# A four-layer fp32 trunk: the pairs' loads in another order, the first layer's squares and the last weights at other places

## Chip, cores, metric

The kernel runs on one core of a Trainium2 chip. The metric is the device time of one execution in microseconds; of several runs the median counts. The engines are called as the profile calls them: PE is TensorE's matmuls (PEld its weight loads), DVE is VectorE, ACT ScalarE, POOL GpSimd, SP SyncE, which here only issues DMAs.

## The reference

One batch of 512 tokens with 1024 channels passes through four residual layers (pool, conv, multi-head latent attention, pool), all in float32. Cut to what matters:

```python
for i in range(4):
    kind, j = i % 3, i // 3
    if kind == 0:
        x = x + pool_mixer(rms_norm(x, pool_norm[j]), ...)
    elif kind == 1:
        x = x + conv_mixer(rms_norm(x, conv_norm[j]), ...)
    else:
        x = x + mla_mixer(rms_norm(x, mla_norm[j]), cos, sin, ...)
return rms_norm(x, final_norm)

def pool_mixer(xn, w_in, w_grp, scale, w_out):
    u, z = split(xn @ w_in, 2)
    ...
    pooled.append(mean - u[:, :, g])
    ...
    mixed = einsum('bsgc,gcd->bsgd', pooled, w_grp) * scale
    return (mixed * silu(z)) @ w_out

def conv_mixer(xn, w_in, conv_w, w_out):
    b, c, h, z = split(xn @ w_in, 4)
    y = b * causal_conv3(c * h, conv_w)
    return (y * silu(z)) @ w_out
```

u, z, b, c and h have 2048 columns each. mean is the trailing mean over the last 2, 4, 8 or 16 tokens, by the column group g.

## The kernel before

**Products.** A matrix product in float32 is made of three matmuls of a shorter type: each operand is split into a high part (a rounded copy, made by ScalarE) and a low part (operand minus high part, made by VectorE), and high x high, high x low and low x high are summed. Names end in h and l for the two parts: wr is a raw block of weights from a DMA, wh and wl are its parts; xh and xl those of the normalised input; yh and yl those of a layer's inner result.

**Jobs.** The work of a layer is a list of jobs (class Stream, L185 to L231). Most jobs load 128x1024 weights, split them (prepare_chunk, L238) and run 24 matmuls of 512 columns: a tile job, for example the u tiles of the pool layers. The other kind is a *pair* (L386 to L460): two tiles of the output from seven products instead of eight, each a product of 12 matmuls of 256 columns. The seven products (function seven, L429) run in the order A11, S1, A22, A12, S2, S4, S3, and need these split weights: ah, al (from the raw block r) for A11 and A22; sh, sl (from s13) for S1 and S3; ch, cl (from r4) for A12; th, tl (from r and r4 after the sums L399 and L400) for S2 and S4. In between, parts of the results are copied out of the accumulators (kept, L440).

A pair's raw data are r (128x1024), r4 (128x512) and s13. s13 is a sum: two loads of the same 128x512 columns into its two halves, and then a DMA on GpSimd's queue that adds the 128x1024 of r's source to it in memory (L120). r and s13 take buffers from the pool "wr", which has four and which also serves the weights of the tile jobs; r4 takes one of two in "wq". A load whose buffer is still in use waits on SyncE's queue, and all loads behind it with it.

**What sets the order.** Inside a stream the order of TensorE, VectorE and ScalarE is the order in which the program issues (tc.manual_schedule, L227); the orders of SyncE and GpSimd are chosen by a scheduler. A job has eight positions, 0 to 7, for a pair the gaps ahead of its products. Steps (functions to be run at a position) are kept in a table (class Steps, L164); a position of 8 or more runs over into the next job. While job j runs, the loads of jobs j+1 and j+2 are issued at its start, and the steps that prepare job j+1's weights lie at its positions: for a pair (L406) 4 ah, 5 al and sh, 6 sl and ch, 7 cl and the sums, 10 th, 11 tl. The steps that take a finished tile further (posts) go to the following jobs. The last pool layer runs its list up to its last eight jobs with all engines' orders left to the scheduler (L1241), and the rest by hand.

**The normalisation.** The input's root mean square is worked out beside the products and applied behind them, as a factor R per token. For it the squares of the eight x tiles are made on ScalarE (L276), summed on GpSimd (the last one on VectorE, L282), closed (split), and turned into the factors by rows (TensorE, VectorE), diagonal (VectorE) and bcast (TensorE), then copied to R (L322). In class Layer (L464) two numbers (at) say after which finished tile rows is put in line, and after which R is made. No tile of the layer can be finished before R is there. A pair needs, beside xh and xl, sums of their halves, the forms (L351): per two x tiles four operations on VectorE (d, L363 to L366), two copies on ScalarE (fh) and two subtractions on VectorE (fl, L382); each forms has its own position.

**The first layer** (pool) starts with two tiles whose matmuls go along with the arrival of x (first_two, L1120). The squares of all eight x tiles then lie in the job behind (positions 0 to 7), close at 10, the four forms at 24, 40, 56 and 72 from there on. rows comes after the fourth tile, R after the sixth (at=(4, 6), L1151). A u tile's post adds shifted copies on GpSimd (L617), up to four of them, then hd, mean and the rest on VectorE (L623 to L625), then a split (plh, pll).

**The end.** The last matrix, pool_out1, is used token-major. Its first column half runs in the last jobs of the stream (token_major, last_half). For its second half four blocks of weights are loaded (L1249) and split into eight parts (wres, L1251 through split, L155 to L162) behind the last job, and then four token tiles follow (L1252 and on), each with its square sums, final norm and its output DMAs.

Of the kernel before, what the change touches and what calls it, by code (L numbers as in the profile page):

```python
# [9 lines left out]
F32 = mybir.dt.float32  # L10
# [6 lines left out]
P = 128  # L17
S = 512
# [46 lines left out]
def trunk_kernel(ctx: ExitStack, tc: tile.TileContext, a):  # L65
# [16 lines left out]
    def wt(s, tag, dt=F32R, w=CH):  # L82
        return wp.tile([P, CH], dt, tag=tag, name=nm(s), bufs=BUFS[tag])[:, :w]
# [29 lines left out]
    def load_pair(src):  # L113

        r, r4, s13 = wt("wr", "wr", F32), wp.tile([P, S], F32, tag="wq", name=nm("wq"), bufs=2), wt("s13", "wr", F32)
        nc.sync.dma_start(r, src[:, :CH])
        nc.sync.dma_start(r4, src[:, CH + S :])
        for q in range(2):
            nc.sync.dma_start(s13[:, q * S : (q + 1) * S], src[:, CH : CH + S])
        nc.gpsimd.dma_start(s13, src[:, :CH], accum_op=ALU.add)  # L120
        return r, r4, s13

# [62 lines left out]
    class Stream:  # L185
# [3 lines left out]
        def __init__(self):  # L189
            self.jobs, self.at, self.later, self.raw, self.ready = [], 0, Steps(), {}, {}  # L190

# [3 lines left out]
        def load(self, j):  # L195
            if j < len(self.jobs) and j not in self.raw:
                kind, src, _ = self.jobs[j]
                self.raw[j] = kind[0](src) if kind else None

# [14 lines left out]
        def step(self):  # L214
            j = self.at
            self.at += 1
            self.load(j + 1)
            self.load(j + 2)
            now, self.later = self.later, Steps()
            now.put(self.prepare(j + 1), 2 if self.jobs[j][0] is PAIR and self.jobs[j + 1 :] and self.jobs[j + 1][0] is not PAIR else 0, first=True)  # L220
            self.jobs[j][2](self.ready.pop(j, None), now)
            now(7)
            left, self.later = self.later, Steps()
            self.later.put(now.at, -8)
            self.later.put(left.at)
# [7 lines left out]
    def load_chunk(src, width=CH):  # L233
        raw = wt("wr", "wr", F32, width)
        nc.sync.dma_start(raw, src)
        return raw

# [14 lines left out]
    def wchunk(src, width=CH, pool=False):  # L252
        w, steps = prepare_chunk(load_chunk(src, width), width, pool)
        Steps(steps)(2)
        return w
# [864 lines left out]
    def first_two():  # L1120

        pre = [ps("pt") for _ in range(2)]
        for k in range(KD):
# [16 lines left out]
            for m in range(2):  # L1140
                wh, wl = w0[m, hf]
                if k == m == 0:
# [4 lines left out]
                    continue  # L1147
                mm3(pre[m], wh[:, c], wl[:, c], *xn0.xs[k], first=(k == 0), last=(k == KD - 1))

        for m in range(KD):  # L1150
            s1.later.put({m: [lambda m=m: xn0.st.add(xt[m])]})  # L1151
        s1.later.put({10: [xn0.st.close]})
        for kk in range(KK):
            s1.later.put(xn0.forms(kk), 24 + 16 * kk)
        return pre

    pool_layer(s1, 0, xn0, half, at=(4, 6), pre=first_two)
    xn = nxt
# [24 lines left out]

    def token_major(stream, c, hf, ys, then):

        pos = []

        def run(wl, now, kp):
            if kp == 0:
                pos.extend(ps("po") for _ in range(NT))  # L1190
# [16 lines left out]
    tail = {}  # L1207

    def last_half(hf, ys):
        if hf == 0:  # L1210
            for c in range(2):
                token_major(s2, c, 0, ys, add_tok)
        else:
            token_major(s2, 0, 1, ys, finish)
            tail["ys"] = ys
# [29 lines left out]
    ys = tail["ys"]  # L1245
    wres = {}
    for kk in range(4):
        raw = wt("wr", "wr", F32)
        nc.sync.dma_start(raw, w[1, 4 + kk])  # L1249
        for e in range(2):  # L1250
            wres[2 * kk + e] = split(raw[:, e * S : (e + 1) * S], "w")  # L1251
    for i in range(NT):  # L1252
# [116 lines left out]
```

## Time and profile before

| | |
|---|---|
| median of 3 runs | 1501.44 us (1498.50 to 1502.46) |
| the profiled execution | 1502.28 us |
| its span, first to last instruction | 1500.5 us |
| mean granted TensorE clock | 0.991 of full speed |
| busy: DVE, ACT, POOL | 1086.7, 686.9, 258.3 us |
| DMA | 181.71 MB, mean 121 GB/s |

The profile shows one execution. A line of the timeline reads: start and duration in us, engine, source line, operation, out<-in by the program's names (s stands for s13 as well as for the sums of the pool layers, since numbers are cut off), shape, and in brackets the idle time of the engine just before, with what ended it. A line of the waits reads: engine and line that waited, what it waited for, us in total, times, and the longest. A line of the windows reads: stretch, its length, busy time (and instructions) of PE, PEld, DVE, ACT and POOL, then the clock granted to TensorE as a share of full speed, the DMA engines' busy share, and GB/s.

### The profile page before, as it was taken

To read this page: it belongs to the slowest core of one execution; us is meant where nothing else is said; L and a number is where in the kernel's file an instruction comes from. 1 tells how busy PE (TensorE), PEld (TensorE's weight loads), DVE (VectorE), ACT (ScalarE), POOL (GpSimd) and SP (SyncE) were. 2 spreads that over 40 slices of the span, in tenths; PEclk is the share of its full clock that TensorE was granted. 3 is DMA by queue.
4 is the path that set the end of the run, shared out by engine and by line. 5 is a ranking of instruction groups with operands and counts; after the bars stand their busy time and mean duration, and the time that the engine had idled before them with its cause. 6 is when DMAs were issued, how large, how long until landed. Compare 5 with 4: busy or idle time off the path is not lost. (4 is left out here: it accounts for less than half of the span.)

```text
span 1500.5 us, 22412 instructions
## 1 busy us (share of the span) xinstructions
PE 1451.2 (97%) x8560; PEld 1273.3 (85%) x8560; DVE 1086.7 (72%) x1771; ACT 686.9 (46%) x1174; POOL 258.3 (17%) x291
## 2 busy tenths in 40 slices
PE   9999999999999999999999999999999999999997
PEld 7788797888999889999879988788888798888886
DVE  5885556659988878998688976667755487655854
ACT  4352233445554425555355655555633355323333
POOL 2413106021001000000211001121201122311502
PEclk9999999999999999999999999999999999999999
DMA  6243354325676457666236642122122434343431
GB/s 229 70 121 105 102 137 99 127 89 120 179 185 162 139 125 191 168 181 194 86 97 169 159 148 74 55 66 84 43 84 85 113 106 115 132 108 117 113 113 57
DMA packets 65147, 181.71 MB, mean 121 GB/s; under 512 B 8080, under 2 KB 8080, under 8 KB 65040
## 3 DMA queue, kind: packets, MB, share of 16 engines
q1 hardware_dynamic: 56688, 151.44, 31.7%
q0 software_dynamic: 7488, 27.27, 10.9%
q8 instruction: 67, 1.10, 0.3%
q10 hardware_dynamic: 864, 1.57, 0.3%
q14 instruction: 40, 0.33, 0.1%
HBM read 173.70 MB, written 2.10 MB: 117 GB/s over the span
## 5 line engine op out<-in xcount | busy, mean ns | idle before, releaser
L248 DVE TENSOR_TENSOR wl<-wr,wh 128x1024 fp32r<-128x1024 f32 (+1 forms) x140 | 173.1, 1236 | 55.9 <-ACT wh L245 54.7
L245 ACT ACTIVATE wh<-wr 128x1024 fp32r<-128x1024 f32 (+1 forms) x140 | 144.4, 1034 | 147.7 <-PE o L259 47.7
L260 PE MATMUL o<-yh,wl 128*128 128x512 f32 x384 | 151.3, 394 | 1.9 <-DVE wl L248 1.9
L259 PE MATMUL o<-yl,wh 128*128 128x512 f32 x384 | 151.3, 394 | 0.2 <-DVE yl L667 0.2
L258 PE MATMUL o<-yh,wh 128*128 128x512 f32 x384 | 150.9, 393 | 0.1
L260 PE MATMUL pt<-xh,wl 128*128 128x512 f32 x367 | 145.3, 397 | 4.0 <-DVE wl L248 4.0
L258 PE MATMUL pt<-xh,wh 128*128 128x512 f32 x367 | 146.2, 398 | 2.7 <-ACT wh L245 2.5
L259 PE MATMUL pt<-xl,wh 128*128 128x512 f32 x367 | 145.2, 396 | 0.6 <-DVE xl L349 0.6
L396 DVE TENSOR_TENSOR sl<-s,sh 128x1024 fp32r<-128x1024 f32 x52 | 65.4, 1259 | 35.2 <-ACT sh L393 32.8
L440 ACT ACTIVATE kept<-bv 128x256 f32<-128x256 f32 x52 | 19.9, 383 | 152.6 <-PE bv L426 90.7
L260 PEld LDWEIGHTS o<-yh,wl 128*128 128x128 f32 x384 | 72.1, 188 | 19.2 <-DVE wl L248 2.8
L260 PEld LDWEIGHTS pt<-xh,wl 128*128 128x128 f32 x367 | 69.5, 189 | 21.6 <-DVE wl L248 5.3
L259 PEld LDWEIGHTS o<-yl,wh 128*128 128x128 f32 x384 | 72.1, 188 | 17.2 <-DVE yl L667 0.5
L258 PEld LDWEIGHTS o<-yh,wh 128*128 128x128 f32 x384 | 72.1, 188 | 17.0 <-ACT yh L664 0.5
L258 PEld LDWEIGHTS pt<-xh,wh 128*128 128x128 f32 x367 | 69.5, 189 | 19.9 <-ACT wh L245 3.8
L259 PEld LDWEIGHTS pt<-xl,wh 128*128 128x128 f32 x367 | 69.5, 189 | 16.5 <-DVE xl L349 1.0
L120 POOL DMA_DIRECT2D s<-in_conv_in x30 | 26.0, 865 | 329.6 <-DMA s<-in_conv_in 105.4
L617 POOL TENSOR_TENSOR s<-u 128x527 f32<-128x527 f32 x32 | 50.0, 1562 | 180.6 <-DVE u L580 146.5
L282 POOL TENSOR_TENSOR sq<-sq,sq 128x512 f32<-128x512 f32 x25 | 39.6, 1585 | 211.3 <-ACT sq L276 210.9
L396 DVE TENSOR_TENSOR al<-wr,ah 128x1024 fp32r<-128x1024 f32 x52 | 64.1, 1233 | 14.2 <-ACT ah L393 12.1
L617 POOL TENSOR_TENSOR s<-s 128x525 f32<-128x525 f32 (+2 forms) x48 | 69.8, 1454 | 14.4 <-PE pm L259 11.1
L393 ACT ACTIVATE sh<-s 128x1024 fp32r<-128x1024 f32 x52 | 54.9, 1055 | 35.1 <-DMA s<-in_conv_in 17.8
(308 smaller groups left out, 4575.2 us busy)
## 6 DMA issues: line engine op xcount, KB each, us to landing
wr<-in_conv_in SPq DMA_DIRECT2D x34, 512.0 KB, 5.6
wr<-in_pool_out SPq DMA_DIRECT2D x32, 512.0 KB, 3.3
wr<-in_pool_u SPq DMA_DIRECT2D x30, 512.0 KB, 3.9
s<-in_conv_in SPq DMA_DIRECT2D x60, 256.0 KB, 4.6
s<-in_conv_in POOLq DMA_DIRECT2D x30, 512.0 KB, 6.2
wr<-in_pool_z SPq DMA_DIRECT2D x18, 512.0 KB, 4.0
wr<-in_pool_grp SPq DMA_DIRECT2D x16, 512.0 KB, 3.3
wr<-in_conv_out SPq DMA_DIRECT2D x16, 512.0 KB, 3.5
```

The source lines that it names most:

```text
L120: nc.gpsimd.dma_start(s13, src[:, :CH], accum_op=ALU.add)
L245: nc.scalar.activation(h, raw, AF.Copy)
L248: (nc.gpsimd if pool else nc.vector).tensor_tensor(out=l, in0=raw, in1=f(h), op=ALU.subtract)
L258: nc.tensor.matmul(out, ah, bh, start=first, stop=False)
L259: nc.tensor.matmul(out, ah, bl, start=False, stop=False)
L260: nc.tensor.matmul(out, al, bh, start=False, stop=last)
L282: eng.tensor_tensor(out=self.sum, in0=self.sum, in1=sq, op=ALU.add)
L393: return lambda: nc.scalar.activation(h, t, AF.Copy)
L396: return lambda: nc.vector.tensor_tensor(out=l, in0=t, in1=f(h), op=ALU.subtract)
L440: nc.scalar.activation(dst, src, AF.Copy)
L617: nc.gpsimd.tensor_tensor(out=nx[:, lo:], in0=cur[:, lo:], in1=cur[:, lo - d : S + PAD - d], op=ALU.add)
```

## The change

It has three parts.

1. **load_pair** issues s13's two loads first, then r and r4, and hands the summing DMA back as a step at position 4 of the job at whose start the loads are issued (Stream.loads), instead of issuing it at once.
2. **The first layer's squares**: first_two adds the square of x tile k-2 while tile k is worked on, the last two at position 0 of the job behind; close moves from position 10 to 3, rows and R one tile ahead (at=(3, 5)), the forms to 48, 56, 64 and 72.
3. **The last weights** (resident): the four loads and eight splits of wres lie at positions of the last four jobs of the stream (loads at 0 or 4, splits from 8, 10 or 12 on), instead of behind the last job. token_major calls resident at the start of each of its jobs, through a new last argument.

The core of the diff:

```diff
-        r, r4, s13 = wt("wr", "wr", F32), wp.tile([P, S], F32, tag="wq", name=nm("wq"), bufs=2), wt("s13", "wr", F32)
+        s13 = wt("s13", "wr", F32)
+        for q in range(2):
+            nc.sync.dma_start(s13[:, q * S : (q + 1) * S], src[:, CH : CH + S])
+        r, r4 = wt("wr", "wr", F32), wp.tile([P, S], F32, tag="wq", name=nm("wq"), bufs=2)
         nc.sync.dma_start(r, src[:, :CH])
         nc.sync.dma_start(r4, src[:, CH + S :])
-        for q in range(2):
-            nc.sync.dma_start(s13[:, q * S : (q + 1) * S], src[:, CH : CH + S])
-        nc.gpsimd.dma_start(s13, src[:, :CH], accum_op=ALU.add)
-        return r, r4, s13
+        return (r, r4, s13), {4: [lambda: nc.gpsimd.dma_start(s13, src[:, :CH], accum_op=ALU.add)]}
...
                 kind, src, _ = self.jobs[j]
-                self.raw[j] = kind[0](src) if kind else None
+                self.raw[j], steps = kind[0](src) if kind else (None, {})
+                self.loads.put(steps)
...
             self.load(j + 2)
             now, self.later = self.later, Steps()
+            now.put(self.loads.at)
+            self.loads = Steps()
...
                 mm3(pre[m], wh[:, c], wl[:, c], *xn0.xs[k], first=(k == 0), last=(k == KD - 1))
-
-        for m in range(KD):
-            s1.later.put({m: [lambda m=m: xn0.st.add(xt[m])]})
-        s1.later.put({10: [xn0.st.close]})
+            if k >= 2:
+                xn0.st.add(xt[k - 2])
+
+        for m in range(KD - 2, KD):
+            s1.later.put({0: [lambda m=m: xn0.st.add(xt[m])]})
+        s1.later.put({3: [xn0.st.close]})
         for kk in range(KK):
-            s1.later.put(xn0.forms(kk), 24 + 16 * kk)
+            s1.later.put(xn0.forms(kk), 48 + 8 * kk)
         return pre
 
-    pool_layer(s1, 0, xn0, half, at=(4, 6), pre=first_two)
+    pool_layer(s1, 0, xn0, half, at=(3, 5), pre=first_two)
     xn = nxt
...
+    wres = {}
+
+    def resident(now, kp):
+
+        for kk, n, at in ((0, 0, 8), (1, 0, 12), (2, 1, 12), (3, 2, 10)):
+            if n == kp:
+                raw = wt("wr", "wr", F32)
+                wres.update({2 * kk + e: (ut("wh", F32R), ut("wl", F32R)) for e in range(2)})
+                now.put({4 if kp else 0: [lambda raw=raw, kk=kk: nc.sync.dma_start(raw, w[1, 4 + kk])]})
+                for e in range(2):
+                    (h, l), half = wres[2 * kk + e], raw[:, e * S : (e + 1) * S]
+                    now.put({at + e: [lambda h=h, half=half: nc.scalar.activation(h, half, AF.Copy)],
+                             at + 2 + e: [lambda h=h, l=l, half=half: nc.vector.tensor_tensor(out=l, in0=half, in1=f(h), op=ALU.subtract)]})
+
     def last_half(hf, ys):
         if hf == 0:
             for c in range(2):
                 token_major(s2, c, 0, ys, add_tok)
         else:
-            token_major(s2, 0, 1, ys, finish)
+            token_major(s2, 0, 1, ys, finish, resident)
             tail["ys"] = ys
...
-    wres = {}
-    for kk in range(4):
-        raw = wt("wr", "wr", F32)
-        nc.sync.dma_start(raw, w[1, 4 + kk])
-        for e in range(2):
-            wres[2 * kk + e] = split(raw[:, e * S : (e + 1) * S], "w")
     for i in range(NT):
         b = slice(i * P, (i + 1) * P)
```

**SyncE in the conv layer.** Ahead of each step in the loop the loads of one pair are queued; wr is r, wq is r4. In the steady part of the conv layer, before:

```order
L116 DMA wr_976_5631<-in_conv_in 128x1024
L119 DMA s13_978_5633<-in_conv_in 128x512 x2
L117 DMA wq_977_5632<-in_conv_in 128x512
L116 DMA wr_995_5764<-in_conv_in 128x1024
L119 DMA s13_997_5766<-in_conv_in 128x512 x2
L117 DMA wq_996_5765<-in_conv_in 128x512
```

and now (line numbers of the changed file):

```order
L117 DMA s13_976_5631<-in_conv_in 128x512 x2
L119 DMA wr_977_5634<-in_conv_in 128x1024
L120 DMA wq_978_5635<-in_conv_in 128x512
L117 DMA s13_995_5764<-in_conv_in 128x512 x2
L119 DMA wr_996_5767<-in_conv_in 128x1024
L120 DMA wq_997_5768<-in_conv_in 128x512
```

s13 and r have changed places in the queue of SyncE; r4 stays the last.

**GpSimd in the first layer.** The summing DMAs of the first layer's last two pairs (s_402 and s_415, in the changed kernel s_400 and s_413) stand among the shifted adds of tiles u31, u32 and u33, four adds to a tile. Before:

```order
L617 TENSOR_TENSOR s_1994<-u_1984 128x527
L617 TENSOR_TENSOR s_1996<-s_1994 128x525
L617 TENSOR_TENSOR s_1998<-s_1996 128x521
L120 DMA s_402_2086<-in_pool_z 128x1024
L617 TENSOR_TENSOR s_2000<-s_1998 128x513
L610 MEMSET u_2081 128x16
L617 TENSOR_TENSOR s_2098<-u_2081 128x527
L617 TENSOR_TENSOR s_2100<-s_2098 128x525
L617 TENSOR_TENSOR s_2102<-s_2100 128x521
L120 DMA s_415_2137<-in_pool_z 128x1024
L617 TENSOR_TENSOR s_2104<-s_2102 128x513
```

and now:

```order
L620 TENSOR_TENSOR s_1954<-s_1952 128x521
L121 DMA s_400_2084<-in_pool_z 128x1024
L620 TENSOR_TENSOR s_1956<-s_1954 128x513
L613 MEMSET u_1984 128x16
L620 TENSOR_TENSOR s_1994<-u_1984 128x527
L620 TENSOR_TENSOR s_1996<-s_1994 128x525
L620 TENSOR_TENSOR s_1998<-s_1996 128x521
L620 TENSOR_TENSOR s_2000<-s_1998 128x513
L613 MEMSET u_2081 128x16
L121 DMA s_413_2135<-in_pool_z 128x1024
L620 TENSOR_TENSOR s_2097<-u_2081 128x527
```

The first of the two has moved ahead by a tile's adds, and the second stands ahead of its tile's first add instead of in front of the last.

**ScalarE in the last layer**, at its last pair but one (z30): ch, sh, th are the splits of the pair's weights, plh that of a u tile, yh that of an inner result, kept the copy behind the pair's second product, gf a load of the final gain. Before:

```order
L393 ACTIVATE sh_14233<-s_2686_14172 128x1024
L393 ACTIVATE ch_14231<-wq_14171 128x512
L628 ACTIVATE plh_14168<-s_14190 128x512
L664 ACTIVATE yh_14260<-E_13889 128x512
L440 ACTIVATE kept_14313<-bv_14310 128x256
L393 ACTIVATE th_14235<-wr_14170 128x512
```

and now:

```order
L396 ACTIVATE sh_14232<-s_2684_14170 128x1024
L443 ACTIVATE kept_14313<-bv_14310 128x256
L396 ACTIVATE th_14234<-wr_14173 128x512
L396 ACTIVATE ch_14230<-wq_14174 128x512
L631 ACTIVATE plh_14168<-s_14189 128x512
L667 ACTIVATE yh_14259<-E_13889 128x512
```

kept and the first th have moved ahead of ch, plh and yh.

More of the change, by code (lines that the diff above doesn't have):

```diff
@@ L189, in __init__ @@
         def __init__(self):
-            self.jobs, self.at, self.later, self.raw, self.ready = [], 0, Steps(), {}, {}
+            self.jobs, self.at, self.later, self.loads, self.raw, self.ready = [], 0, Steps(), Steps(), {}, {}
         def add(self, kind, src, run):
@@ L235, in load_chunk @@
         nc.sync.dma_start(raw, src)
-        return raw
+        return raw, {}
     def prepare_chunk(raw, width=CH, pool=False):
@@ L252, in wchunk @@
     def wchunk(src, width=CH, pool=False):
-        w, steps = prepare_chunk(load_chunk(src, width), width, pool)
+        w, steps = prepare_chunk(load_chunk(src, width)[0], width, pool)
         Steps(steps)(2)
@@ L1182, in trunk_kernel, with token_major @@
     w = a["pool_out1"]
-    def token_major(stream, c, hf, ys, then):
+    def token_major(stream, c, hf, ys, then, stay=None):
         pos = []
         def run(wl, now, kp):
+            if stay:
+                stay(now, kp)
             if kp == 0:
```

## The prediction

> **What bounds the kernel now.** I read the busy shares of the page first, then TensorE's waits, then the windows (for the granted clock), and last the timeline around each wait that the change can reach.
>
> ```profile
> span 1500.5 us, 22412 instructions
> PE 1451.2 (97%) x8560; PEld 1273.3 (85%) x8560; DVE 1086.7 (72%) x1771; ACT 686.9 (46%) x1174; POOL 258.3 (17%) x291
> 1440.00:1460.00 20.00, 20.00 (x88) 16.22 (x87) 8.39 (x10) 4.86 (x6) 0.00 (x0) 1.00 0.33 106
> ```
>
> TensorE is the bound: busy for 97% of the span. At its steady pace it starts 88 matmuls of 512 columns in 20 us, one each 0.23, so that a job of 24 lasts 5.5 us. The change leaves the matmuls as they are. It can win only the places where TensorE waits, and lose only by making new ones. Its parts reach four groups of waits: in the pairs of the conv and attention layers (380 to 900 us), in the first layer's opening (60 to 95), near 250, and near 1469. A fifth place, near 1414, has a changed order of ScalarE.
>
> **Part 1, the pairs' loads: s13 asked for ahead of r.** First TensorE's waits from 380 to 900 us on the tiles made of s13, then SyncE's waits for a buffer over the span, then one pair of the conv layer.
>
> ```profile
> PE bx L426 <- DVE tl L396: 3.0, 7, 1.0
> PE bv L426 <- DVE sl L396: 2.2, 3, 0.8
> PE bv L420 <- ACT sh L393: 1.8, 2, 1.0
> ...
> SPq L116 <- DVE wr L399: 170.2, 32, 10.6
> SPq L119 <- DVE tl L396: 84.6, 32, 4.7
> ...
> 411.11 0.86 POOL L120 DMA_DIRECT2D s<-in_conv_in  x1 [9.93 <-DVE cl L396]
> 411.47 0.33 SPq L116 DMA_DIRECT2D wr<-in_conv_in  x1
> 414.70 1.08 SPq L119 DMA_DIRECT2D s<-in_conv_in  x2
> 420.22 1.06 ACT L393 ACTIVATE sh<-s 128x1024 fp32r<-128x1024 f32 x1 [3.50 <-DMA s<-in_conv_in]
> 421.33 0.38 PE L420 MATMUL bv<-fh,sh 128*128 128x256 f32 x1 [0.78 <-ACT sh L393]
> 427.43 1.04 ACT L393 ACTIVATE ah<-wr 128x1024 fp32r<-128x1024 f32 x1
> ...
> 1412.66 0.28 PE L425 MATMUL bv<-fl,sh 128*128 128x256 f32 x1
> 1412.78 0.28 PE L426 MATMUL bv<-fh,sl 128*128 128x256 f32 x1
> ```
>
> The summing DMA of this pair's s13 went out at 411.11, and its sum was there when sh began at 420.22, 9.1 us later. ScalarE had then stood 3.50 for it, and TensorE 0.78 for sh. The three rows of waits give 7.0 us in 12 waits. Each understates its loss: steady matmuls of 256 columns start 0.12 apart and are recorded as 0.28 long (the last two rows, from a pair that nothing holds up), so a shown gap hides 0.16 more. That makes 7.0 + 12 x 0.16 = 8.9 us.
>
> In the loop r waits for a buffer until the sums of an earlier pair (L399) are done, s13 until its tl (L396), which comes later; here 411.47 against 414.70, 3.2 us apart. With s13 asked for first, the two trade places: s13 goes out about 3.2 us earlier and r about as much later. The longest stand of sh here, 3.50, then shrinks to some 0.3, and since TensorE stood only 0.78 of that, its wait goes. I keep 0.9 of the 8.9 for pairs where a sum is slow again: gain **8.0** (range 4 to 8.9).
>
> What the move costs: r is now the later of the two. It is first read by ah, at 427.43 for the r that would be asked for at 414.70, so it has 12.7 us.
>
> ```profile
> wr<-in_conv_in SPq DMA_DIRECT2D x34, 512.0 KB, 5.6
> DMA to landing us min/median/max: 5.4/6.2/9.1
> ```
>
> r lands in 5.6 us (first row); even the slowest summing DMA, of the same 512 KB, took 9.1 (second row). That leaves 3.6 us, so r's delay is hidden behind the products of the pair before, and costs nothing. If the cover were gone, ah would come late and with it the first product of each pair (a rival below). The summing DMA's later place in the program costs nothing either: GpSimd stands for s13's loads anyway, and in the conv layer its queue keeps its order.
>
> **Part 1 in the first layer, near 250.** GpSimd's queue among the adds for tile u32, VectorE's step behind them, TensorE's wait, and two windows (the granted clock is the third number from the end):
>
> ```profile
> 248.41 0.87 POOL L120 DMA_DIRECT2D s<-in_pool_z  x1 [1.93 <-DMA s<-in_pool_z]
> 250.64 0.17 DVE L623 TENSOR_TENSOR hd<-s,con 128x16 f32<-128x16 f32 x1 [4.48 <-POOL s L617]
> 254.49 0.39 PE L426 MATMUL bx<-xh,al 128*128 128x256 f32 x1 [3.26 <-DVE al L396]
> ...
> 254.98:258.40 3.42, 3.42 (x19) 3.42 (x18) 3.42 (x4) 0.63 (x1) 2.51 (x2) 0.50 0.00 0
> 380.00:690.00 310.00, 303.99 (x2358) 292.47 (x2358) 267.01 (x376) 157.09 (x257) 24.02 (x39) 1.00 0.64 167
> ```
>
> The summing DMA sits inside the adds and holds GpSimd for 1.93 until the loads have landed; hd, then al, then TensorE wait in a chain. In the changed order it stands ahead of these adds, with its loads asked for earlier. So hd comes 1.93 sooner and TensorE's wait falls from 3.26 to 1.3. The window behind the wait had a granted clock of 0.50 for 3.42 us, which costs 1.7. A wait of 2.06 near 1469 (below) was followed by such a window too, while the conv layer, 380 to 690, with single waits of up to 1.0 (above), kept 1.00. At 1.3 I take the clock to stay whole: gain 1.9 + 1.7 = **3.6** (range 1.9, if the clock still falls, to 5.1, if the whole wait goes). [...]
>
> **Part 2, the last weights.** Around the wait for their first split:
>
> ```profile
> 1445.84 1.21 DVE L248 TENSOR_TENSOR wl<-wr,wh 128x1024 fp32r<-128x1024 f32 x1
> 1469.42 7.03 DVE L161 TENSOR_TENSOR wl<-wr,wh 128x512 fp32r<-128x512 f32 x8 [0.37 <-ACT wh L158]
> 1469.44 1.52 PE L258 MATMUL po<-wh,yh 128*128 128x512 f32 x5 [2.06 <-ACT wh L158]
> ...
> 1470.13:1473.54 3.41, 3.17 (x10) 2.31 (x9) 3.41 (x4) 2.90 (x6) 2.16 (x2) 0.50 0.01 2
> ```
>
> The eight splits stand in a row behind the squares of the row sums (L1224), and TensorE waits 2.06 for the first, then runs 3.41 us at half clock (1.7). Moved into the last four jobs, they need 7.0 us of VectorE in a stretch where it is busy 8.39 of 20, and ScalarE 4.86 (window 1440 to 1460, above). They fit. Gain 2.06 + 0.16 + 1.7 = **3.9** (range 2.2, if the clock still falls for another reason, to 4.2). What they move back: on SyncE's queue two of the new loads now stand ahead of the chunk of the last job, which so waits for the buffer that the split at 1445.84 frees, until 1447. Its load, 512 KB like those above, would land by 1453; its job is the last of four of 5.5 us before 1465, so it has until 1460. Nothing is lost.
>
> **Part 3, the first layer's squares.** TensorE's waits from 60 to 95 us, a window, and VectorE's rows:
>
> ```profile
> PE pt L260 <- DVE wl L248: 3.2, 2, 2.4
> PE pt L258 <- ACT wh L245: 1.6, 2, 1.3
> PE pm L260 <- DVE wl L248: 0.7, 1, 0.7
> ...
> 60.00:80.00 20.00, 15.16 (x53) 10.99 (x51) 19.62 (x34) 7.86 (x12) 9.88 (x9) 0.83 0.17 57
> ...
> 26.65 0.69 DVE L282 TENSOR_TENSOR sq<-sq,sq 128x512 f32<-128x512 f32 x1 [8.06 <-POOL sq L282]
> 37.88 0.47 DVE L363 SCALAR_TENSOR_TENSOR d<-x,par,g 128x256 f32<-128x256 f32 x1
> 39.58 1.47 DVE L382 TENSOR_TENSOR fl<-d,fh 128x512 fp32r<-128x512 f32 x2
> ```
>
> TensorE loses 5.5 + 5 x 0.16 = 6.3 here and, by the clock of 0.83 over 20 us, 0.17 x 20 / 2 = 1.7 more: 8.0 in all. VectorE is why: 19.62 of 20 us busy, behind with the splits wl. It had idled 8.06 at 26.65 for GpSimd's sums of squares. The change ends that, and R comes one job (5.5 us) sooner. But it also moves all four sets of forms (3.2 us of VectorE each, 37.88 to 41.05) into four jobs from about 58 on, where two of the four now lie earlier, outside the crowded stretch: 2 x 3.2 = 6.4 more work there against 5.5 us of earlier start. So I keep the two waits for wl (3.2) and the clock's 1.7, and let the others go: 1.6 + 0.7 + 3 x 0.16 = 2.8. I take off 0.4 for the new squares beside VectorE's first splits: gain **2.4** (range -1 to 8.0).
>
> **The order near 1414.** In the last layer kept and the first th now stand ahead of ch on ScalarE.
>
> ```profile
> 1406.61 0.63 ACT L393 ACTIVATE ch<-wq 128x512 fp32r<-128x512 f32 x1 [1.02 <-POOL s L617]
> 1413.79 0.36 ACT L440 ACTIVATE kept<-bv 128x256 f32<-128x256 f32 x1
> 1414.31 0.28 PE L420 MATMUL bv<-xh,ch 128*128 128x256 f32 x1
> 1418.32 0.38 PE L426 MATMUL bx<-fh,tl 128*128 128x256 f32 x1 [1.92 <-DVE tl L396]
> ```
>
> kept needs TensorE's second product, whose last matmul is the one at 1412.78 above, done near 1413.1. Then come kept (0.36) and th (a split of 128x512 like ch, 0.63), so that ch begins near 1414.1 and ends near 1414.7; cl on VectorE needs some 0.7 more (as long as the 128x512 sum at 26.65), 1415.4. TensorE wants ch at 1414.31 and cl 0.23 later: up to 0.9 late, and plh and yh, pushed back likewise, can move 1418's wait by as much. Cost **1.0** (range a gain of 1, if the early th helps tl, to a cost of 3).
>
> **Sum.** 8.0 + 3.6 + 3.9 + 2.4 - 1.0 = 16.9 us. The profiled execution took 1502.28, so 1485.4; the median of the runs shown, 1501.44, is 0.84 lower, so **1484.5**. A measurement of this kernel tells some 0.3%, 4.5 us, from no change.
>
> **Rivals.**
> - *The opening's backlog goes altogether.* VectorE's 8.06 of idling is more than the 6.4 that is added. Then 8.0 instead of 2.4: 1478.9. Against it, the forms and the late splits still meet in the same jobs. Chance 0.15.
> - *The pairs win nothing.* The change does not do there what it says: s13 goes out sooner, but its summing DMA then runs beside r's load and takes the time back. For it: the one that was late took 9.1, the median is 6.2. Then 1484.5 + 8.0 = 1492.5. Chance 0.14.
> - *The squares' sums block VectorE in the opening.* Now they run beside the first splits. VectorE's hd of 16 columns took 1.03 beside such an add, 0.17 alone:
>
> ```profile
> 58.99 1.03 DVE L623 TENSOR_TENSOR hd<-s,con 128x16 f32<-128x16 f32 x1
> 17.92 8.69 POOL L282 TENSOR_TENSOR sq<-sq,sq 128x512 f32<-128x512 f32 x6 [16.87 <-ACT sq L276]
> ```
>
>   If each of the six adds held VectorE for its whole 1.45, and the first two tiles waited for it, 8.7 us would be lost: 1484.5 + 8.7 = 1493.2. Against it: TensorE's first two tiles pace only the last xl. Chance 0.08. [...]
> - *Slower: r becomes the late one.* r is now the last to be asked for. If it lands over 12.7 us after its issue, ah and the first product of all 52 pairs wait. To end over 0.3% slower this must eat 16.9 + 4.5 = 21.4 us, 0.41 a pair, so a landing of 13.1 or more; at 13.2 it costs 52 x 0.5 = 26, and the time is 1510.5. Against it: no row above 9.1. Chance 0.03.
> - The forecast keeps 0.60.
>
> **How the numbers follow.** The unknown terms' bounds, mainly -1 to 8.0 in the opening and 4 to 8.9 in the pairs, give about 1476 to 1492 around 1484. With the two rivals at 1492.5 and 1493.2 and the one at 1478.9 inside, and a little for two misses at once, the range is 1476 to 1494; the fourth rival and double misses are left out. Slower: 0.03. Within 0.3% (1497 to 1506): both of those rivals together with a bad opening, 0.05. Faster: 0.92.
>
> **What would show it.** Right: sh's waits for its DMA gone, s13 issued at the time r had; hd's wait near 250 shorter by about 2 and the granted clock there whole; no TensorE wait for wh at the start of the last token tiles; VectorE's 8.06 wait gone and R one job sooner. Wrong: waits of ah or al on r's DMA, long xl in the first 17 us, splits wl still late at two or more places after 60, or a TensorE wait for ch or cl near 1414 that halves the clock.

## The result, and the profile after

The changed kernel takes **1491.37 us** (median of 4 runs, 1489.86 to 1492.30), the kernel before 1501.95 beside it (4 runs, 1498.50 to 1505.50): a ratio of **0.9929** (95% interval 0.9910 to 0.9947), faster by some 10.6 us. 1484.5 was forecast, with 1476 to 1494.

To see where the time went, I follow the same matmul through the traces: the first matmul `bx<-xh,ah` of a pair, at six places, and the end of the span. The table has how many us earlier than in the kernel before each of them starts (the columns are its times there; a step from one column to the next is what that stretch gave or took).

| us earlier at | 95.90 | 197.56 | 355.27 | 866.53 | 1200.40 | 1410.05 | 1423.97 | end, 1500.51 |
|---|---|---|---|---|---|---|---|---|
| the changed kernel | -2.4 | -1.6 | -3.4 | +7.1 | +10.5 | +10.7 | +6.6 | +10.9 |

So the opening took 1.6; the end of the first layer (with the wait near 250) took 1.8; the conv and attention layers gave 10.4; the stretch from there to the last layer gave 3.4, of which the prediction does not speak; the pair near 1410 took 4.0; and the end gave 4.2. Two of the five terms of the sum came out (the pairs of conv and attention, which gave more than forecast, and the last weights), three did not. The table sets one execution against one other; how far executions differ is said with experiments 1 to 3.

The page's first lines of the changed kernel, TensorE's waits from 345 to 860 us, SyncE's waits for a buffer, and one pair of the conv layer (line numbers are now 3 to 4 higher: L396 is the splits' ScalarE line, L399 their VectorE line, L117 s13's loads, L119 r's, L121 the summing DMA):

```profile
span 1489.6 us, 22425 instructions
PE 1445.5 (97%) x8560; PEld 1272.1 (85%) x8560; DVE 1088.9 (73%) x1771; ACT 683.9 (46%) x1174; POOL 256.3 (17%) x291
...
PE bx L429 <- DVE tl L399: 2.5, 3, 1.0
...
SPq L117 <- DVE wr L402: 200.1, 32, 11.1
SPq L119 <- DVE tl L399: 64.0, 32, 4.2
...
404.71 0.80 SPq L117 DMA_DIRECT2D s<-in_conv_in  x2
407.20 0.33 SPq L119 DMA_DIRECT2D wr<-in_conv_in  x1
409.89 0.86 POOL L121 DMA_DIRECT2D s<-in_conv_in  x1 [8.94 <-ACT kept L443]
419.64 1.05 ACT L396 ACTIVATE sh<-s 128x1024 fp32r<-128x1024 f32 x1
```

s13 and r have traded their waits as forecast: s13 now waits for the sums (L402), r for tl. sh starts without a wait: this pair's sum landed at 416.36, 3.3 ahead of it. The waits for sl and sh are gone from the list. Of the three for tl that are left two lie ahead of 380 us, at the conv layer's first pairs, and one in the attention layer; from 380 to 690 the view lists no wait of TensorE at all.

The first layer near 250: SyncE, GpSimd, VectorE, TensorE, and the clock behind the wait.

```profile
242.26 0.80 SPq L117 DMA_DIRECT2D s<-in_pool_z  x2
247.66 0.88 POOL L121 DMA_DIRECT2D s<-in_pool_z  x1 [8.33 <-DMA s<-in_pool_z]
248.27 1.37 POOL L620 TENSOR_TENSOR s<-u 128x527 f32<-128x527 f32 x1
253.32 0.18 DVE L626 TENSOR_TENSOR hd<-s,con 128x16 f32<-128x16 f32 x1 [4.97 <-POOL u L613]
257.16 0.58 PE L429 MATMUL bx<-xh,al 128*128 128x256 f32 x1 [3.79 <-DVE al L399]
257.00:261.00 4.00, 3.84 (x18) 3.84 (x19) 4.00 (x5) 0.63 (x1) 3.16 (x2) 0.50 0.00 0
256.00:264.00 8.00, 6.84 (x36) 6.84 (x37) 7.96 (x10) 2.68 (x5) 4.14 (x2) 0.57 0.19 62
```

The summing DMA left its place inside u32's adds, but it now stands in front of the first of them, and holds GpSimd there until s13's loads have landed: the first add starts right behind it, at 248.27. hd still waits, 4.97 (4.48 in the kernel before), and TensorE 3.79 (3.26). Behind it the clock is at 0.50 for some 6.8 us, as the last window's mean of 0.57 over 8 us says (0.43 x 8 x 2); in the kernel before it was 3.4. So only some 0.5 of the 1.8 lost is a longer wait, and most of the rest is the second stretch at half clock.

The last layer's pair near 1410, in the same way; ch is the split on ScalarE whose place had changed.

```profile
1388.39 0.88 POOL L121 DMA_DIRECT2D s<-in_pool_z  x1 [4.44 <-PE pt L262]
1391.77 0.17 DVE L626 TENSOR_TENSOR hd<-s,con 128x16 f32<-128x16 f32 x1 [4.14 <-POOL u L613]
1402.18 0.17 DVE L626 TENSOR_TENSOR hd<-s,con 128x16 f32<-128x16 f32 x1 [3.36 <-POOL s L620]
1403.18 0.62 ACT L396 ACTIVATE ch<-wq 128x512 fp32r<-128x512 f32 x1
1403.92 0.92 DVE L628 TENSOR_TENSOR s<-hd,u 128x16 f32<-128x16 f32 x1
1404.76 0.68 DVE L399 TENSOR_TENSOR cl<-wq,ch 128x512 fp32r<-128x512 f32 x1
1405.50 0.38 PE L429 MATMUL bv<-xh,cl 128*128 128x256 f32 x1 [1.15 <-DVE cl L399]
1408.11 0.38 PE L423 MATMUL bx<-fh,th 128*128 128x256 f32 x1 [1.17 <-ACT kept L443]
1410.53 0.58 PE L429 MATMUL bx<-fh,tl 128*128 128x256 f32 x1 [1.92 <-DVE tl L399]
1400.00:1420.00 20.00, 15.68 (x103) 14.85 (x103) 15.82 (x21) 7.64 (x13) 7.67 (x7) 0.83 0.19 58
```

ch is ready at 1403.80, but cl starts only at 1404.76, right behind the row of L628, the end of hd's chain on VectorE. hd had waited 3.36 for GpSimd's adds (1.05 in the kernel before). These had begun late because their tile u came late from VectorE, whose queue had stood 4.14 for the hd of the tile before, behind the summing DMA at 1388.39. (The row of that DMA names PE, but its s13's loads, issued at 1379.58, had landed only at 1387.83, and it went out as soon behind them as the one near 250.) TensorE waits 1.15 and 1.17 more than before, beside the 1.92 that was there, and the clock of 0.83 over 20 us is 6.8 us at 0.50. In the kernel before it was half of that, 0.83 over 10 us:

```profile
1414.00:1424.00 10.00, 8.06 (x54) 7.65 (x53) 9.38 (x13) 5.74 (x10) 1.77 (x2) 0.83 0.31 105
```

The two new waits and the second stretch, 1.15 + 1.17 + 1.7, are the 4.0.

The opening, VectorE first, then ScalarE and TensorE:

```profile
13.93 5.04 DVE L352 SCALAR_TENSOR_TENSOR xl<-x,par,xh 128x512 fp32r<-128x512 f32 x3
22.38 0.69 DVE L285 TENSOR_TENSOR sq<-sq,sq 128x512 f32<-128x512 f32 x1 [1.18 <-POOL sq L285]
62.50 1.28 DVE L366 SCALAR_TENSOR_TENSOR d<-x,par,g 128x256 f32<-128x256 f32 x1
...
38.64 0.60 ACT L325 ACTIVATE R<-pr 128x512 f32<-128x512 f32 x1 [11.12 <-PE pr L323]
70.64 0.63 ACT L631 ACTIVATE plh<-s 128x512 fp32r<-128x512 f32 x1 [1.59 <-DVE s L628]
71.18 1.04 ACT L248 ACTIVATE wh<-wr 128x1024 fp32r<-128x1024 f32 x1
...
62.63 0.50 PE L263 MATMUL pt<-xh,wl 128*128 128x512 f32 x1 [1.41 <-DVE wl L251]
72.27 0.80 PE L261 MATMUL pt<-xh,wh 128*128 128x512 f32 x1 [4.31 <-ACT wh L248]
60.00:80.00 20.00, 14.24 (x48) 10.36 (x47) 19.16 (x34) 8.61 (x14) 6.61 (x6) 0.83 0.19 53
```

VectorE's wait for the sums of squares fell from 8.06 to 1.18, but three xl now take 5.04; in the kernel before they took 2.07 at the same place:

```profile
13.93 2.07 DVE L349 SCALAR_TENSOR_TENSOR xl<-x,par,xh 128x512 fp32r<-128x512 f32 x3
```

Later, too, little is won: VectorE is still full from 60 to 80 (19.16 of 20). The wait moved: wh stands behind plh on ScalarE, plh behind VectorE's chain, and TensorE waits 4.31 at 72.27.

The end is as forecast: from 1455 to 1475, where the token tiles begin now, TensorE runs without a gap at full clock.

```profile
1455.00:1475.00 20.00, 20.00 (x89) 16.26 (x88) 7.29 (x17) 5.25 (x14) 6.97 (x6) 1.00 0.07 27
```

### The profile page after: what moved, and what is told of

The parts are those of the page before. It is cut to its first block, busy times and chain, and to the rows that moved or that the text cites. A ratio compares the mean times of both kernels' runs of the same rounds, so it can differ in the third digit from the quotient of the medians.

```text
span 1489.6 us, 22425 instructions
## 1 busy us (share of the span) xinstructions
PE 1445.5 (97%) x8560; PEld 1272.1 (85%) x8560; DVE 1088.9 (73%) x1771; ACT 683.9 (46%) x1174; POOL 256.3 (17%) x291
## 3 DMA queue, kind: packets, MB, share of 16 engines
q0 software_dynamic: 7488, 27.27, 10.6%
## 5 line engine op out<-in xcount | busy, mean ns | idle before, releaser
L399 DVE TENSOR_TENSOR sl<-s,sh 128x1024 fp32r<-128x1024 f32 x52 | 64.6, 1242 | 22.2 <-ACT sh L396 22.2
L121 POOL DMA_DIRECT2D s<-in_conv_in x30 | 26.2, 873 | 309.6 <-DVE cv L724 67.6
L399 DVE TENSOR_TENSOR al<-wr,ah 128x1024 fp32r<-128x1024 f32 x52 | 64.1, 1233 | 15.4 <-ACT ah L396 13.3
L620 POOL TENSOR_TENSOR s<-s 128x525 f32<-128x525 f32 (+2 forms) x48 | 66.2, 1379 | 14.7 <-PE pm L262 11.3
L443 ACT ACTIVATE kept<-bx 128x512 f32<-128x512 f32 x104 | 51.0, 491 | 37.8 <-PE bx L429 37.8
```

Of the source, the lines that this page charges most:

```text
L121: return (r, r4, s13), {4: [lambda: nc.gpsimd.dma_start(s13, src[:, :CH], accum_op=ALU.add)]}
L399: return lambda: nc.vector.tensor_tensor(out=l, in0=t, in1=f(h), op=ALU.subtract)
L443: nc.scalar.activation(dst, src, AF.Copy)
L620: nc.gpsimd.tensor_tensor(out=nx[:, lo:], in0=cur[:, lo:], in1=cur[:, lo - d : S + PAD - d], op=ALU.add)
```

## Experiments

My theory after the traces: the five places are worth what the table shows, each from its own part, and the losses near 250 and 1410 come from the summing DMA's place in GpSimd's queue. The rivals are named with each run. A ratio is to the kernel before, on the same chip; "us earlier" is as in the table above. Line numbers in a run's rows are those of its own kernel.

**1 to 3. Each part alone.** The pairs' loads only (the hunks of load_pair and Stream), the squares only (first_two and at), the last weights only (resident). The gist of each:

```diff
-        r, r4, s13 = wt("wr", "wr", F32), ...
+        s13 = wt("s13", "wr", F32)
...
-    pool_layer(s1, 0, xn0, half, at=(4, 6), pre=first_two)
+    pool_layer(s1, 0, xn0, half, at=(3, 5), pre=first_two)
...
-            token_major(s2, 0, 1, ys, finish)
+            token_major(s2, 0, 1, ys, finish, resident)
```

> Only the pairs' loads are changed (part 1); squares and last weights stand as before. By the ledger of the two traces (offset of the same pair's first product, after minus before): the conv layer gives 10.4 us, the end of the first layer takes back 1.8, the last layer's z30 takes back 4.0, the attention layer's pairs give 0, so 1501.9 - 4.6 = 1497.3 (1495 to 1499), and the wait of al near 250 and those near 1405 are there as in the changed kernel. The rival that these two losses come from the other parts (squares moved, so that the layer stands otherwise on the clock's stretches; last weights in the queue) says 1501.9 - 10.4 = 1491.5 and no wait at either place longer than before's.

> Only the first layer's squares, rows, R and forms are moved (part 3). Ledger: the first pair starts 2.4 us later than before, the second 1.7 later: 1501.9 + 1.6 = 1503.5 (1502 to 1505). The rival, that the moved squares are worth what was forecast (2.4) and the loss of the opening came from the pairs' loads in SyncE's queue there, says 1499.5.

> Only the last weights are moved (part 2). Ledger: 4.2 us after the last pair, so 1501.9 - 4.2 = 1497.7 (1496.5 to 1499); TensorE's wait for wh at the last token tiles gone, no half clock there. The rival, that half of these 4.2 us belong to another stand of the clock's stretches, says 1499.8.

| | median us (runs), before | ratio (95%) | 95.90 | 197.56 | 355.27 | 866.53 | 1200.40 | 1410.05 | 1423.97 | end |
|---|---|---|---|---|---|---|---|---|---|---|
| pairs only | 1493.54 (11), 1500.25 (28) | 0.9951 (0.9935 to 0.9968) | -0.1 | +0.4 | -0.5 | +9.5 | +11.2 | +11.3 | +8.4 | +8.7 |
| squares only | 1502.06 (12) | 1.0013 (0.9991 to 1.0035) | -2.6 | -1.8 | -2.6 | +0.6 | +2.3 | +2.0 | +3.6 | +1.8 |
| last weights only | 1495.67 (12) | 0.9971 (0.9954 to 0.9988) | +0.4 | +0.4 | +0.3 | -2.7 | -0.9 | -0.7 | -0.6 | +3.7 |

The loss near 1410 is there with the pairs' loads alone (2.9) and with neither of the other parts. Near 250 it is less clear: the pairs' loads lose 0.9 there, but the squares alone, with the summing DMA at its old place, lose 0.8 too (TensorE's wait for al is 3.5, and the clock is at 0.50 for some 6.8 us behind it, as in the changed kernel: 0.90 from 240 to 275 in both). The whole part gives 6.7 us by the medians, 2.1 more than I expected. The squares lose 2.6 at the first pair by themselves and are worth nothing in time (the interval takes in 1). The last weights give 4.3 behind 1423.97, and the time agrees (4.6 by the medians).

Something else shows: with the old loads the conv and attention layers differ from one execution to the next (from 355.27 to 866.53 the squares alone gain 3.2, the last weights alone lose 3.0, though neither touches these layers); with the new loads the same stretch gives 9.0 to 10.8 in each of the ten traces that have them (experiment 12 aside, where another thing costs 7.7 us there). TensorE's waits for sl, sh and tl between 345 and 870 are 7.0 and 8.5 us with the old loads in these two runs, and 2.5 with the new ones in the first.

**4. Old loads in the pool layers.**

```diff
+    def load_pair_now(src):
+        ...
+        nc.gpsimd.dma_start(s13, src[:, :CH], accum_op=ALU.add)
+        return (r, r4, s13), {}
...
-        ly = Layer(xn, at, 3 if pre is None else 6)
+        ly = Layer(xn, at, 3 if pre is None else 6, NOW)
```

> The changed kernel, but the pairs of the two pool layers load as before (r, r4, s13); those of the conv and attention layers keep the new order. If the summing DMAs that now stand ahead of the shifted adds in GpSimd's queue cost the 1.8 us near 250 and the 4.0 near 1405, both go: 1491.4 - 5.8 = 1485.6 (1484 to 1488), with the two places as in the kernel before (they lost 5.3 and 4.1 there, at half clock). The rival, that these places lose because everything ahead of them was shifted against the clock's stretches and the squares' work came later, leaves 1491.

1487.97 us (6 runs; before 1500.25), ratio 0.9913 (0.9890 to 0.9937). The interval overlaps that of the changed kernel, so the times alone don't separate the two; the trace does near 1410: +10.9 there and +11.2 behind it, so the 4.0 are back. Near 250 only part came back (from -1.4 at 197.56 to -2.0 at 355.27, 0.6 instead of 1.8), and the wait for al is 4.1, longer than the changed kernel's 3.8; what came back is the second stretch at half clock, which is not there in this execution (a clock of 0.95 from 240 to 275 instead of 0.90). So by the wait the old place of the summing DMA near 250 is as bad as the new one. One thing is lost by it: the changed kernel gains 1.5 near 1190, since there the old order has the summing DMA in front of sr, a step of the normalisation, on GpSimd's queue:

```profile
1191.10 0.87 POOL L120 DMA_DIRECT2D s<-in_pool_z  x1 [12.44 <-DMA s<-in_pool_z]
1191.66 1.37 POOL L300 TENSOR_TENSOR sr<-sv,mhalf 128x4 f32<-128x4 f32 x1
```

(kernel before; in the changed one the DMA is out long before, and sr waits for its input alone).

**5 and 6. Where the forms stand.** On the kernel of experiment 4:

```diff
-            s1.later.put(xn0.forms(kk), 48 + 8 * kk)
+            s1.later.put(xn0.forms(kk), 24 + 16 * kk)
...
+            s1.later.put(xn0.forms(kk), (4, 15, 64, 72)[kk])
```

> The kernel with the pool layers' old loads (ratio 0.9913 to before), and the four sets of forms back at 24, 40, 56 and 72. If the four sets, pushed into four jobs in a row, ate what the earlier R had won, TensorE's waits from 60 to 90 us (6.6 us and a stretch at half clock) shrink to some 3 and the time falls by about 4 (ratio 0.9885). The rival, that GpSimd's adds beside VectorE are what makes the splits late wherever the forms stand, says no change (ratio 0.9905 to 0.992).

> The same with the first two sets of forms moved ahead of R (positions 4 and 15), where VectorE stands 3.2 and 4.9 us now, and the last two at 64 and 72 as in the changed kernel. If the forms make the splits wl late, the waits at 62 and 72 us go with the half clock behind them: 6 to 8 us, ratio 0.986 to 0.9875. The rival of GpSimd's adds says that the waits stay, some 1 us less, ratio 0.9905.

The forms at their old places: 1491.85 us (6 runs; before 1501.13, 11 runs), ratio 0.9934 (0.9911 to 0.9957), and the first pair starts 5.9 us later than before, 3.7 later than in experiment 4. My theory that their later places had eaten the gain falls: with R earlier, the old places lie in the midst of the posts, and TensorE waits 6.1 for wl and 3.4 for wh up to 100 us. Two sets ahead of R: 1483.01 us (4 runs), ratio 0.9881 (0.9856 to 0.9906); the first pair starts 1.6 earlier than before, 3.8 earlier than in experiment 4. VectorE fits them where it stood idle:

```profile
24.94 0.48 DVE L376 SCALAR_TENSOR_TENSOR d<-x,par,g 128x256 f32<-128x256 f32 x1
27.79 1.29 DVE L395 TENSOR_TENSOR fl<-d,fh 128x512 fp32r<-128x512 f32 x2
29.38 0.29 DVE L308 CUSTOM_DVE_ANT_0 sd<-st,con 128x128 f32<-128x128 f32 x1 [0.31 <-PE st L304]
```

So it is VectorE's work in the crowded stretch that decides, and the cure is to take it out of there, not to shift it within. Half of what I expected of this run came, 3.8 of 6 to 8 at the first pair (4.8 by the ratios): waits of 1.41 for wl near 62 and 1.5 for wh are left.

**7 and 8. What the squares cost.** On the kernel of experiment 4, the first layer's squares summed on VectorE; and that kernel without any of the squares' part.

```diff
-                eng = nc.vector if self.i == self.n else nc.gpsimd
+                eng = nc.vector if self.i == self.n or self.dve else nc.gpsimd
```

> The same as the kernel with the pool layers' old loads, but the first layer's squares are summed on VectorE, six sums of 0.69 more there, none on GpSimd. If GpSimd's sums slow VectorE's xl and wl in the first 22 us (1.68 each instead of 0.75), the 1.9 us lost there shrink to 0.5 or less, ratio 0.9903. The rival, that ScalarE's squares stand in the way of xh, leaves the 1.9 us and adds VectorE's 4.1: ratio 0.992 to 0.994.

> The new loads in the conv and attention layers and the last weights, without any of the squares' part. By the squares alone (ratio 1.0013 to before, and the first pair 2.6 us later in the trace, the second 1.9) this gains 1.7 to 2 against the kernel with the squares: ratio 0.990. If the squares' part is worth something that the first pair does not show, 0.9915 or more.

Sums on VectorE: 1488.03 us (6 runs, 1483.79 to 1490.91), ratio 0.9912 (0.9888 to 0.9936): no difference in time from experiment 4 that can be told, while the trace shows the first pair 2.2 us earlier (0.0 against -2.2), and xl undisturbed:

```profile
15.02 0.75 DVE L362 SCALAR_TENSOR_TENSOR xl<-x,par,xh 128x512 fp32r<-128x512 f32 x1
15.68 0.69 DVE L295 TENSOR_TENSOR sq<-sq,sq 128x512 f32<-128x512 f32 x1
```

0.75 for an xl, against 5.04 / 3 = 1.68 beside GpSimd's sums. Without the squares' part: 1487.20 us (5 runs), ratio 0.9909 (0.9886 to 0.9931), the first pair at -0.4, the second column at +0.1. By the trace the squares' part, as it is in the change, costs 1.5 to 1.8 us at these two places; in time the difference to experiment 4 is too small to be told.

**9. Both repairs**, experiments 6 and 7 together.

> Pool layers with their old loads, the first two sets of forms ahead of R, and the first layer's squares summed on VectorE. If the two repairs add up (3.8 us at the first pair from the forms, 2.2 in the first 20 us from the sums): ratio 0.9865 to 0.988, the first pair some 3.7 us earlier than in the kernel before. The rival, that VectorE's six sums now push back the forms put ahead of R and eat the second gain, leaves 0.9881.

**1480.13 us** (4 runs, 1479.42 to 1481.29; before 1500.02, 7 runs), ratio **0.9869** (0.9853 to 0.9885). The first pair starts 5.3 us earlier than before; from experiment 4's -2.2 the two repairs' sum of 3.8 and 2.2 would have been +3.8. The other 1.5 is about what a stretch of 3.41 us at half clock costs, 1.7: from 60 to 80 the clock is 0.83 in the changed kernel and in experiment 7, 0.91 in 6, and 1.00 here.

```profile
60.00:80.00 20.00, 17.52 (x73) 13.40 (x74) 18.88 (x33) 9.22 (x14) 5.21 (x5) 1.00 0.24 79
```

This version beats both kernels.

**10. No summing DMA in the pool layers**, on the changed kernel (in load_pair_now, s13 first):

```diff
-        return (r, r4, s13), {4: [lambda: nc.gpsimd.dma_start(s13, src[:, :CH], accum_op=ALU.add)]}
+        return (r, r4, s13), {}
```

> The changed kernel, with the summing DMA of the 14 pairs of the pool layers left out (so their s13 is not the sum), s13 still loaded first. If that DMA, waiting in GpSimd's queue ahead of the shifted adds, is what makes al late near 250 and cl and tl late near 1405, hd comes some 2 to 4 us earlier there, and the 4.1 us near 1405 and over 1 of the 1.9 near 250 are gone: 1491.4 - 5 = 1486. The rival, that ScalarE's order (kept and th ahead of ch) makes cl late near 1405, keeps that loss, since ScalarE's order does not depend on it: 1490.

1483.07 us (4 runs; before 1500.02), ratio 0.9888 (0.9868 to 0.9908). From 197.56 to 355.27 the kernel goes from -1.3 to +1.8, a gain of 3.1 where the changed one lost 1.8, and behind 1410.05 from +12.8 to +15.7, a gain of 2.9 where it lost 4.0. Near 250 hd waits 1.54 instead of 4.97, and the wait for al is all but gone (TensorE's waits from 230 to 275):

```profile
PE bx L439 <- DVE tl L409: 0.8, 1, 0.8
PE bx L439 <- DVE al L409: 0.4, 1, 0.4
```

So the summing DMA in GpSimd's queue is the cause of the waits at both places, in the changed kernel and, near 250, in the one before. The run does not part this from ScalarE's order near 1410, since without that DMA the scheduler puts ch ahead of kept again; there the rows above decide, in which ch was ready 0.96 us ahead of cl's start.

**11. r behind r4** in the conv and attention layers, on the kernel of experiment 4:

```diff
-        nc.sync.dma_start(r, src[:, :CH])
         nc.sync.dma_start(r4, src[:, CH + S :])
+        nc.sync.dma_start(r, src[:, :CH])
```

> The kernel with the pool layers' old loads, and in the conv and attention layers s13, r4, r: r behind r4 too, about 1 us later. If r has several us in hand (12.7 against a landing of 4.4 to 5.6), nothing moves: ratio 0.9913 within 0.002, no wait of ah or al on r's DMA. The rival, that r is the next late one, shows waits of ah on r's DMA in most pairs and up to 0.5 us a pair: ratio 0.925 to 0.999 is to be read as at least 0.995.

1487.24 us (4 runs), ratio 0.9917 (0.9899 to 0.9934), as experiment 4; TensorE's waits in these layers are the same (2.5 for tl, 1.1 for al against 1.0), and no ah waits for r's DMA. The rival of a late r is out, with at least that much to spare. (The rival's range in the expectation is misprinted; its last words hold.)

**12. The summing DMA really behind the adds.** In the change its step at position 4 moves nothing: with the DMA issued at once the program has the same order on every queue, since GpSimd's is the scheduler's. Here, on experiment 9, that order is by hand too:

```diff
-ORDERED = {mybir.EngineType.PE, mybir.EngineType.DVE, mybir.EngineType.Activation}
+ORDERED = {mybir.EngineType.PE, mybir.EngineType.DVE, mybir.EngineType.Activation, mybir.EngineType.Pool}
...
+        return (r, r4, s13), {6: [lambda: nc.gpsimd.dma_start(s13, src[:, :CH], accum_op=ALU.add)]}
```

> The kernel with both repairs, GpSimd's order now by hand too, and the pool layers' summing DMA at position 6 of the job at whose start its loads are issued: on GpSimd's queue it now stands behind the last shifted add of a tile instead of among or ahead of the adds. If its place among the adds makes hd and al late near 250 (6.5 us lost there) and cl and tl near 1415 (4), most of both goes, 6 to 9 us: ratio 0.981 to 0.9835. The rival, that the sum now lands too late for sh of those pairs, puts a wait of sh on the DMA in the place of the old wait: ratio 0.986 to 0.99.

1488.24 us (6 runs; before 1502.79, 11 runs), ratio 0.9902 (0.9877 to 0.9927): 5 us worse than experiment 9 by the ratios. The rival was right in what it said of sh: near 250 hd is on time, but the sum lands at the last moment, and TensorE waits 2.70 for sh where it waited 3.8 for al, so that the stretch from 197.56 to 355.27 loses 0.3 instead of 0.6. Near 1410 nothing is won. The 5 us are lost elsewhere: GpSimd's order by hand holds the DMA back in the attention layer's first pair as well, where its step stands at position 4, and TensorE waits there for sh (3.12) and sl (1.87), behind which its matmuls of 256 columns start 0.21 apart instead of 0.12 up to 788.56. Between that pair and the next the lead over the kernel before falls from 15.2 to 7.6. The run changes both things at once, so it does not price the place behind the adds alone.

```profile
249.98 0.58 PE L432 MATMUL bv<-fh,sh 128*128 128x256 f32 x1 [2.70 <-ACT sh L405]
781.52 0.39 PE L432 MATMUL bv<-fh,sh 128*128 128x256 f32 x1 [3.12 <-ACT sh L405]
```

## Why the prediction was right or wrong

- **The total** fell inside the range partly by luck. Three terms together came out 12.4 lower than forecast (near 250 by 5.4, the opening by 4.0, near 1414 by 3.0). The pairs gave 2.4 more, and 3.4 came from a place that the prediction does not speak of. Without these 5.8 the time would have been some 1497, outside the range.
- **The pairs of conv and attention: right** in mechanism, and larger than its own range of 4 to 8.9: +10.4 for 8.0. s13 and r trade their buffers' waits, sh is never late, r has time to spare (experiment 11). From 355.27 to 866.53 TensorE's listed waits fall from 12.1 us in 19 to 6.2 in 9, with the 0.16 for each 7.5 of the 10.4; the other 2.9 stand in no wait that the view lists. How much the old loads lose also varies between executions (experiments 2 and 3), so one trace does not fix the size.
- **The last weights: right**, 4.2 for 3.9 (experiment 3), and the half clock there went with the wait (1.00 from 1416.60 to 1488.00).
- **Near 250: wrong**, -1.8 for +3.6. The step that failed: "So hd comes 1.93 sooner". I took the wait away from the place where the DMA had stood, and did not put it back at the place where it stands now: ahead of the same tile's first add, where it holds the whole chain until s13's loads have landed. That these loads would be there by then was my assumption; they were issued at 242.26, because their buffer was freed only by a split wl. Experiment 10 shows the DMA to be the cause, experiment 4 that by the wait the old place was no better. The clock did not stay whole either: it was at 0.50 for twice as long as before, 6.83 us instead of 3.41.
- **Near 1414: right in sign only**, -4.0 for -1.0, outside the term's range. The step named ScalarE's order, and gave nothing for the clock. The rows show VectorE's order: cl, with ch ready at 1403.80, starts at 1404.76 behind hd's chain, hd behind GpSimd's adds, these behind the summing DMA. The change in ScalarE's order was a sign of the DMA's move, not the cause.
- **The opening: wrong**, -1.6 for +2.4. Two steps failed. "I take off 0.4 for the new squares" should have been some 2.2 (experiment 7): GpSimd's sums more than double the time of each xl (1.68 beside them, 0.75 without). And "let the others go": the waits for wh, 1.6 in all, did not go but grew to one of 4.31, since ScalarE's wh stands behind a plh that VectorE makes late. That the forms were the trouble was half right: too much of VectorE's work was due between 57 and 83, but their old places would be worse (experiment 5); ahead of R two of them cost TensorE at most some 0.4 (experiment 6: 2.0 behind the kernel before at 58 us, experiment 4 1.6). One working of this part is too small: a clock of 0.83 over 20 us is 3.4 us lost, not 1.7, if TensorE has work throughout. It had not: of the two stretches at 0.50 in the kernel before (67.25 to 70.67 and 70.67 to 74.08) it was busy 1.72 and 3.41 us, so the loss was some 2.6. The 2.4 does not use this term, the 8.0 of its range and of the first rival does.
- **Not foreseen:** 3.4 between 866.53 and 1200.40. 1.5 of it is a wait near 1194 that was there in the kernel before (the row below) and is gone: sr, freed from the summing DMA by the pool layers' new loads, is followed by dg, for which TensorE waited (in experiment 4, with the old loads, it waits 1.1 again):

```profile
PE pr L319 <- DVE dg L313: 1.5, 1, 1.5
```

  The rest lies in the attention itself, which the change does not touch: a wait of 2.39 there had been followed by a half-clock stretch (0.50 from 944.48 to 947.89), and is 1.88 now without one (1.00 from 930 to 950). It is no gain of the change: the squares alone and the last weights alone have the wait near 1194 still (1.2), and yet gain 1.7 and 1.9 in this stretch. The wait in the attention is 2.9 in experiment 12. Why it varies stays open.
- **The rivals:** the opening's backlog did not go (19.16 of 20 us). That the pairs win nothing is refuted by experiment 1; its reason was half right, for the summing DMAs land later now, by the median 7.1 us instead of 6.2, but still ahead of sh. The squares' sums did disturb VectorE, at a quarter of the price that the rival set (2.2 of 8.7). A late r is refuted. Of the signs of being wrong three came: long xl in the first 17 us, splits wl late at two places after 60 (1.8 us in all), and a wait for cl at z30's pair (1405.50), with half clock behind the two waits that follow it (0.50 from 1409.70 to 1416.53). The step at position 4 does nothing, as the unchanged order shows; the load order did all the work.

## What to carry to other kernels

A DMA that waited in GpSimd's own queue was here a wait of everything behind it (near 250 GpSimd stood idle 8.33 ahead of one, with a tile's four adds behind it): when such an instruction moves, ask what stands behind its new place, and whether its data are there by then, before counting the old wait as won. Issue what a sum needs first where buffers come free one after the other. And where an engine is full in one stretch, moving work earlier helped here only where it landed in a gap of that engine (the first pair 3.8 us earlier in experiment 6 than in 4, 3.7 later in experiment 5): look for that gap in its rows first.

## What the runs showed of the hardware

- The granted clock: between 10 and 1480 us it was 0.50 in the kernel before for 6.83 us from 67.25 and for 3.41 from 254.98, 930.82, 944.48, 1418.93 and 1470.13; in the changed kernel for 6.83 from 71.67, 255.99 and 1409.70 and for 3.41 from 925.01; elsewhere 1.00. The length of a wait alone does not say whether such a stretch follows: a wait of 1.92 near 1418 in the kernel before was followed by one, the wait of 1.9 for tl at this place in experiment 2 was not (1.00 from 1385 to 1425). What parts the two is not shown.
- Operations of VectorE beside adds of GpSimd: xl 1.68 (changed kernel, 13.93) instead of 0.75 (experiment 7, 15.02); d of 128x256 1.28 at 62.50 instead of 0.48 at 66.22, behind the last of the adds there (both in the changed kernel).
- The kernel before spread over 1494.8 to 1508.0 us in 28 runs, the pairs' part alone over 1493.0 to 1496.9 in 11, the best version over 1479.4 to 1481.3 in 4. The new loads in conv and attention seem to narrow it, but not by themselves: experiment 7, which has them, went from 1483.8 to 1490.9 in 6.
